# One transformer layer on one core: fewer seven-product groups in two weight blocks, and quarter sums moved from GpSimd to VectorE

## The chip, the core and the metric

The kernel runs on one core of a Trainium2 chip. The core has a matrix engine (TensorE, PE in the profile; its weight loads are PEld), three elementwise engines (VectorE = DVE, ScalarE = ACT, GpSimd = POOL), a queue engine that only issues transfers here (SyncE = SP), and 16 DMA engines that all queues share. The metric is the device time of one execution in microseconds, lower is better. Times below are from one profiled execution of the kernel before, and from three timed runs of it.

## The reference, cut to what matters

All arrays are float32. The sequence has 256 tokens, the model is 2048 wide, the feed-forward part 5632. The attention and retention heads are left out here, since the change does not touch them: `mixed` stands for what they give.

```
n = rmsnorm(h, norm_mix_w);  proj = n @ w_in
mixed = concat(attention(proj), retention(proj))     # 256 x 2048
h  = h + mixed @ w_out                               # 2048 x 2048
n2 = rmsnorm(h, norm_ffn_w)
h  = h + (silu(n2 @ w_gate) * (n2 @ w_up)) @ w_down  # 2048 x 5632, twice, and 5632 x 2048
y  = rmsnorm(h, norm_final_w)
```

## The kernel before

**Precision by halves.** Each float32 operand is split into a rounded part and the rest. A weight tile of 128 x 1024 is copied by ACT into the rounded half of a `ws` tile, and DVE subtracts to get the rest (`halved`, lines 529 to 532). PE then multiplies high with high, high with low and low with high, so every product is three matmuls (`three`, line 574). Five `ws` buffers exist.

**Blocks.** From 367 us on, the program is a row of blocks. Each multiplies the 256 tokens with a weight block of 1024 output columns: `o0` and `o1` for w_out, `gu0` to `gu10` for 512 columns of w_gate beside 512 of w_up, and `d0_0` to `d2_1` for w_down, in three groups. A block has 16 slices of 128 rows of the weights (12 in `d2_0` and `d2_1`). It is computed in two ways:

- An item `C` takes one slice classically: two halves of the tokens by two halves of the columns, 12 matmuls of 128 x 512, adding to the four results that are called 2, 3, 4 and 8 (PSUM banks).
- Four slices can be taken together by seven products in the manner of Strassen, items `1` to `7` of 6 matmuls each: 42 matmuls in place of 48. The letter `a` is the first four slices, `b` the next four. Item 1 loads three weight tiles, item 2 a fourth. Some products need sums of weight tiles: DVE adds two of them in place (`rawt`), and two are made by a DMA of POOL's queue that adds while it writes (`plus`, line 534). So seven tiles have to be halved, not four.

`M` (`mid`, line 666) combines the products 1, 5, 6 and 7 into four parts of 128 x 512, one ACT copy and four DVE operations. In `o0` and `o1` these parts are added to the residual `ht` by four DMAs of POOL's queue; in the `gu` blocks they stay. When a result's last matmul is done, one DVE operation of 128 x 512 ends it (`end_out`, `end_gu`); in `o0` and `o1` it needs the DMA of its part to have landed, and ACT then takes the sum of its squares.

**Activations.** `T` turns 128 x 512 pieces onto the feature axis: 8 transposes on PE, then copies to two tiles. In `o1` the two T's make `n2` of `ht0` and `ht1` (`turn_n2`), in `gu0` those of `ht2` and `ht3`, in later blocks T turns the gated output of the block before (`h2`). `H` gates: silu on ACT, one product on DVE. The seven products need sums of quarters of the activations as well, of 128 x 128 each (`pair_sums`, line 539): s5 = a22 - a21, s2 = a11 + s5, s3 = a11 - a21, s4 = a12 - s2. POOL makes these four, and the result `s` is halved into `sa`. That happens for the four tiles of the two T's in `o1`, and for two tiles in each of `gu1`, `gu2`, `gu5`, `gu6` and `gu9`: 14 tiles, 56 operations.

**What sets the order.** A string for each kind of block (`ORDERS`, lines 33 to 40) gives the order of its items by hand. `ch` chains each engine's instructions of the block stage in just this order. Before item k runs, the loads and halvings of the items up to three ahead have been written to the queues (`AHEAD = 3`). Work put on the list `later` (squares, the halving of `s`) is taken off one per item, behind the item. Raw weight tiles come from rings of buffers by home: three `rawc` (all C items and each item 1), three `raw22`, two `raw12`, one `rawt`. All loads are issued by SP in order, and a load waits until its buffer was read for the last time.

Of the kernel before, what the change touches and what calls it, by code (L numbers as in the profile page):

```python
# [12 lines left out]
ALU = mybir.AluOpType  # L13
# [4 lines left out]
S = 256  # L18
# [12 lines left out]
AHEAD = 3  # L31
MAIN = "1a 5a H 2a C T 3a C 6a C 7a 1b C 4a 5b C 2b 6b C 7b M C C 3b 4b"
ORDERS = {
# [3 lines left out]
    "main": MAIN,  # L37
    "short": "1a 5a H 2a C T 3a C 6a C 7a C M C 4a C C C",
    "final": "1a 5a 2a C 3a C 6a C 7a M C 4a K K K K Z",
# [49 lines left out]
def encoder_layer(ctx: ExitStack, tc: tile.TileContext, xT, x, gains, gain_f, decay, tab, w_qk, w_in, w_st, y):  # L89
# [8 lines left out]
    nc = tc.nc  # L98
# [10 lines left out]
    def atile(name):  # L109
        return actp.tile([P, 2, 2, S], F32R, tag="act", name=name)  # L110

    def ttile(name):
        return tmp.tile([P, 2, S], F32, tag="tmp", name=name)
# [152 lines left out]
    for c in range(KT // 2):  # L266
# [10 lines left out]
        a = atile(f"n1_{c}")  # L277
# [223 lines left out]
    queue, later = {}, []  # L501

    def ch_ins(ins):

        if ins.engine in queue:
            tc.add_manual_dep(
                ins, queue[ins.engine].name,
                mybir.DependencyInfo(mybir.DependencyClass.NoSync, mybir.DependencyReason.DATA), reason="stream",
            )
        queue[ins.engine] = ins  # L510

    def ch(ins):
        ch_ins(ins.ins)
# [9 lines left out]
    def copy(out, src, func=AF.Copy, **kw):  # L523
        ch(nc.scalar.activation(out, src, func, **kw))  # L524

    def tt(out, x, y, op):
        ch(nc.vector.tensor_tensor(out, x, y, op=op))  # L527

    def halved(to, src):

        copy(to[:, :, 0, :], src)
        tt(to[:, :, 1, :], src, to[:, :, 0, :].bitcast(F32), ALU.subtract)
# [6 lines left out]
    def pair_sums(t, name):  # L539
        s = ttile(f"s_{name}")  # L540
        a11, a21, a12, a22 = (t[:, f, i * P:(i + 1) * P] for f in range(2) for i in range(2))
        s5, s2, s3, s4 = (s[:, f, i * P:(i + 1) * P] for f in range(2) for i in range(2))
        for out, p, q, op in ((s5, a22, a21, ALU.subtract), (s2, a11, s5, ALU.add),
                              (s3, a11, a21, ALU.subtract), (s4, a12, s2, ALU.subtract)):
            ch(nc.gpsimd.tensor_tensor(out, p, q, op=op))  # L545
        a = atile(f"sa_{name}")
        later.append(lambda: halved(a, s))
        return a

    flat = "p f t -> p (f t)"  # L550
# [133 lines left out]
    def turn(t, name, dst, w=None, sums=None):  # L684

        for p in range(2):
            pt = halves(ps1(f"pt_{name}{p}"))
            for f in range(2):
                for i in range(2):
                    ch(nc.tensor.transpose(pt[:, f, i * P:(i + 1) * P], t(i)[:, (2 * p + f) * P:(2 * p + f + 1) * P], ident))  # L690
            a = atile(f"{name}_{p}")
            c = len(dst)
            dst.append(a)
            if sums is not None:
                o = ttile(f"o_{name}{p}")
                if w is None:
                    copy(o, pt)
                else:
                    for f in range(2):
                        copy(o[:, f], pt[:, f], scale=w[:, 2 * c + f:2 * c + f + 1])  # L700
                halved(a, o)
                sums.append(pair_sums(o, f"{name}_{p}"))
            elif w is None:
                halved(a, pt)
            else:
                for f in range(2):
                    g = w[:, 2 * c + f:2 * c + f + 1]
                    copy(a[:, f, 0, :], pt[:, f, :], scale=g)
                    ch(nc.vector.scalar_tensor_tensor(
                        a[:, f, 1, :], pt[:, f, :], g, a[:, f, 0, :].bitcast(F32), op0=ALU.mult, op1=ALU.subtract  # L710
                    ))
# [79 lines left out]
    for g, (lo, hi, s) in enumerate(GROUPS):  # L791
        h2, s2 = [], []
# [104 lines left out]
```

## Time and profile before

| what | value |
|---|---|
| median of three runs | 1191.64 us (1189.43 to 1192.74) |
| the profiled execution | 1192.01 us, of which the profile's span 1190.0 us |
| PE busy in the span | 96% |
| DVE busy | 82% |
| ACT, POOL busy | 57%, 21% |
| DMA engines, mean busy share in the slices of the block stage | 0.5 to 0.9 |
| input projection and heads | 0 to 367 us |
| `o0`, `o1`, `gu0` (by PE's first matmul) | from 367.0, 410.0, 459.1 us |
| `gu1` and the rest | from 518.4 us |

The span runs from the first to the last instruction that the profile shows; the 2.0 us beside it are outside the profile. Tile names are given without buffer numbers: `p_gu` is any of the result banks of any gu block, `raw_gu` a raw tile of the homes 22 and 12. In a timeline row the first number is the start in us, the second the time that the row takes, `x6` the number of instructions merged into it, and the bracket the idle time of the engine before it and what ended that.

### The profile page before, as it was taken

The page shows a single profiled execution, that of the slowest core. Times are in us where ns is not written, and L with a number is a line of the kernel's source. Part 1 is how long each engine was busy: PE and PEld are TensorE (multiplying, and loading weights), DVE is VectorE, ACT ScalarE, POOL GpSimd, SP SyncE. Part 2 cuts the span into 40 slices and gives each one's busy share as a digit, 9 for nine tenths or more (in the row PEclk, how much of TensorE's full clock was granted, in tenths as well). Part 3 has the DMA queues.
Part 4 walks back from the last instruction along what each step waited for, and adds up shares of the span by engine and source line. Part 5 has one row for each costly group of instructions (what it writes and reads, how often), then busy time and mean ns, then how long its engine had stood idle before and what let it go on. Part 6 is the DMA issues. An engine that isn't in the chain of part 4 may idle for free.

```text
span 1190.0 us, 15290 instructions
## 1 busy us (share of the span) xinstructions
PE 1140.6 (96%) x5534; PEld 950.0 (80%) x5534; DVE 977.8 (82%) x1007; ACT 681.2 (57%) x830; POOL 255.8 (21%) x258
## 2 busy tenths in 40 slices
PE   7999999999999987899999999999999999999996
PEld 5888888888887775677788878778788878878885
DVE  8887787667687787789898889789999878989985
ACT  5455555555555574546666645566666655656653
POOL 8332322203122251031300022032100112121011
PEclk9999999999999998899999999999999999999998
DMA  8665565554556968768788899978897899979785
GB/s 319 208 228 160 178 195 165 157 185 157 184 168 178 261 186 226 218 187 254 217 260 247 274 248 260 311 204 258 258 255 233 250 295 254 276 247 287 239 229 143
DMA packets 77691, 269.47 MB, mean 226 GB/s; under 512 B 8880, under 2 KB 8880, under 8 KB 77616
## 3 DMA queue, kind: packets, MB, share of 16 engines
q1 hardware_dynamic: 61920, 221.29, 53.8%
q0 software_dynamic: 14976, 46.14, 21.8%
q10 hardware_dynamic: 720, 1.07, 0.2%
q8 instruction: 43, 0.70, 0.2%
q14 instruction: 32, 0.26, 0.1%
HBM read 220.23 MB, written 2.10 MB: 187 GB/s over the span
## 4 chain that ended last, share of the span: by engine, by line
PE 74%; DVE 8%; DMA 6%; issue 4%; POOL 3%; ACT 3%; SPq 0%; DVEq 0%; POOLq 0%; ACTq 0%
PE p_gu L578 30%; PE p_d L578 15%; PE ps_qr L157 3%; PE ps_gr L157 3%; PE ps_vr L164 2%; PE ps_kr L157 2%; POOL s_h L545 2%; PE ps_va L164 2%; PE p_o L578 2%; PE ps_ka L157 2%; DVE ws_gu L527 2%; DMA rawc_d<-in_w_st 2%; DMA ht<-part_o 2%; PE ps_qa L157 2%; ACT ws_gu L524 1%
## 5 line engine op out<-in xcount | busy, mean ns | idle before, releaser
L578 PE MATMUL p_gu<-ws_gu,n 128*128 128x512 f32 x1452 | 352.0, 393 | 12.3 <-DVE ws_gu L527 9.0
L578 PEld LDWEIGHTS p_gu<-ws_gu,n 128*128 128x128 f32 x1452 | 273.7, 189 | 76.8 <-DVE ws_gu L527 14.7
L578 PE MATMUL p_d<-ws_d,h 128*128 128x512 f32 x708 | 168.6, 390 | 2.2 <-DVE ws_d L527 1.5
L578 PEld LDWEIGHTS p_d<-ws_d,h 128*128 128x128 f32 x708 | 132.8, 188 | 31.0 <-DVE ws_d L527 2.1
L527 DVE TENSOR_TENSOR ws_gu<-rawc_gu,ws_gu 128x1024 fp32r<-128x1024 f32 x110 | 134.4, 1222 | 26.1 <-ACT ws_gu L524 24.3
L524 ACT ACTIVATE ws_gu<-rawc_gu 128x1024 fp32r<-128x1024 f32 x110 | 115.7, 1056 | 49.1 <-PE p_gu L578 26.4
L578 PE MATMUL p_gu<-ws_gu,sa_n 128*128 128x512 f32 x528 | 136.4, 394 | 6.9 <-DVE ws_gu L527 4.4
L578 PEld LDWEIGHTS p_gu<-ws_gu,sa_n 128*128 128x128 f32 x528 | 98.9, 189 | 28.1 <-DVE ws_gu L527 4.7
L527 DVE TENSOR_TENSOR ws_gu<-raw_gu,ws_gu 128x1024 fp32r<-128x1024 f32 x88 | 107.5, 1222 | 5.5 <-ACT ws_gu L524 3.6
L524 ACT ACTIVATE ws_gu<-raw_gu 128x1024 fp32r<-128x1024 f32 x88 | 92.8, 1054 | 32.0 <-PE p_gu L578 24.0
L527 DVE TENSOR_TENSOR ws_d<-rawc_d,ws_d 128x1024 fp32r<-128x1024 f32 x54 | 65.7, 1220 | 18.9 <-ACT ws_d L524 18.1
L524 ACT ACTIVATE ws_gu<-rawt_gu 128x1024 fp32r<-128x1024 f32 x44 | 46.5, 1056 | 58.9 <-DVE rawt_gu L527 49.4
L524 ACT ACTIVATE ws_d<-rawc_d 128x1024 fp32r<-128x1024 f32 x54 | 57.2, 1059 | 35.5 <-PE p_d L578 18.9
L537 POOL DMA_DIRECT2D raw_gu<-raw_gu x22 | 19.1, 868 | 222.8 <-DVE rawt_gu L527 208.8
L578 PE MATMUL p_d<-ws_d,sa_h 128*128 128x512 f32 x240 | 61.2, 390 | 0.0
L527 DVE TENSOR_TENSOR ws_gu<-rawt_gu,ws_gu 128x1024 fp32r<-128x1024 f32 x44 | 53.7, 1220 | 5.6 <-ACT ws_gu L524 5.6
L578 PEld LDWEIGHTS p_d<-ws_d,sa_h 128*128 128x128 f32 x240 | 44.8, 188 | 9.2
L524 ACT ACTIVATE ws_d<-raw_d 128x1024 fp32r<-128x1024 f32 x40 | 42.3, 1056 | 14.2 <-PE p_d L578 12.7
L527 DVE TENSOR_TENSOR ws_d<-raw_d,ws_d 128x1024 fp32r<-128x1024 f32 x40 | 48.8, 1219 | 0.8
L578 PE MATMUL p_o<-ws_o,mr 128*128 128x512 f32 x192 | 46.6, 391 | 2.0 <-DVE ws_o L527 2.0
L537 POOL DMA_DIRECT2D raw_gu<-rawt_gu x22 | 19.0, 862 | 135.9 <-DVE ws_gu L527 135.9
L164 PE MATMUL ps_va<-ws_va,n 128*128 128x512 f32 x128 | 45.8, 400 | 0.0
(258 smaller groups left out, 2343.9 us busy)
## 6 DMA issues: line engine op xcount, KB each, us to landing
rawc_gu<-in_w_st SPq DMA_DIRECT2D x110, 512.0 KB, 5.4
raw_gu<-in_w_st SPq DMA_DIRECT2D x66, 512.0 KB, 5.5
rawc_d<-in_w_st SPq DMA_DIRECT2D x58, 512.0 KB, 4.9
raw_d<-in_w_st SPq DMA_DIRECT2D x30, 512.0 KB, 4.9
raw_gu<-raw_gu POOLq DMA_DIRECT2D x22, 512.0 KB, 7.6
raw_gu<-rawt_gu POOLq DMA_DIRECT2D x22, 512.0 KB, 5.7
rawc_o<-in_w_st SPq DMA_DIRECT2D x20, 512.0 KB, 4.5
raw_va<-in_w_in SPq DMA_DIRECT2D x16, 512.0 KB, 4.3
```

The source lines that it names most:

```text
L157: nc.tensor.matmul(ps[:, f, :], t[:, j, 0, f * P:(f + 1) * P], a, start=start, stop=False)
L164: nc.tensor.matmul(ps[:, f, :], a[:, 0, f * P:(f + 1) * P], t[:, j, :, :], start=first, stop=False)
L524: ch(nc.scalar.activation(out, src, func, **kw))
L527: ch(nc.vector.tensor_tensor(out, x, y, op=op))
L537: ch(nc.gpsimd.dma_start(out, other, accum_op=ALU.add))
L545: ch(nc.gpsimd.tensor_tensor(out, p, q, op=op))
L578: ch(nc.tensor.matmul(self.bank(r), x[u], w[v], start=r not in self.begun, stop=self.left[r] == 0))
```

## The change

Three things are edited.

First, in the strings of `o1` and `gu0` (kinds `out1` and `gu_first`) the seven products of the second four slices go, and four C items take their place: 7 products and 12 C items in a block, where there were 14 and 8. Each of the two blocks has 186 matmuls of 128 x 512 then, where it had 180, and 19 halvings and 2 DVE sums of weight tiles, where it had 22 and 4; two of the four DMA sums go as well. The T's and `M` stand at other places between the items. Second, the items of `o0` are the same ones in another order: `M` has 7 items behind it, not 4. Third, `pair_sums` does its four operations on DVE (by `tt`), and they are put on `later`, ahead of the halving of `s`.

```diff
-    "out0": "1a 5a 2a 3a S 6a 7a S 1b C 4a C 5b C 2b C 6b C 7b C M 3b C 4b C",
-    "out1": "1a 5a 2a C T 3a C T C 6a C 7a 1b 4a C 5b 2b C 6b C 7b M C 3b 4b",
-    "gu_first": "1a 5a 2a T 3a T 6a 7a 1b C 4a 5b C 2b C 6b C 7b C M C C 3b C 4b",
+    "out0": "1a 5a 2a 3a S 6a 7a S 1b C 5b 4a 6b C 2b C 7b M C 3b C C 4b C C",
+    "out1": "1a 5a 2a C 3a C T 6a C 7a C M C 4a C T C C C C C C",
+    "gu_first": "1a 5a 2a C T C C T C 3a 6a C 7a C 4a M C C C C C C",
...
     def pair_sums(t, name):
         s = ttile(f"s_{name}")
...
-        for out, p, q, op in ((s5, a22, a21, ALU.subtract), (s2, a11, s5, ALU.add),
-                              (s3, a11, a21, ALU.subtract), (s4, a12, s2, ALU.subtract)):
-            ch(nc.gpsimd.tensor_tensor(out, p, q, op=op))
         a = atile(f"sa_{name}")
-        later.append(lambda: halved(a, s))
+
+        def add():
+            for out, p, q, op in ((s5, a22, a21, ALU.subtract), (s2, a11, s5, ALU.add),
+                                  (s3, a11, a21, ALU.subtract), (s4, a12, s2, ALU.subtract)):
+                tt(out, p, q, op)
+
+        later.extend([add, lambda: halved(a, s)])
         return a
```

The first place is the seam from `o1` to `gu0` on DVE. `part..` is the work of `M`, `ht..` the four ends of `o1`, `ws_gu0` the halvings of gu0's first items. Before:

```order
L527 TENSOR_TENSOR v_o1_4086<-part0_o1_4082,p6_o1_3937 128x512
L674 SCALAR_TENSOR_TENSOR part2_o1_4084<-p5_o1_3767,v_o1_4086 128x512
L527 TENSOR_TENSOR part1_o1_4083<-p7_o1_3966,v_o1_4086 128x512
L527 TENSOR_TENSOR part3_o1_4085<-part2_o1_4084,p7_o1_3966 128x512
L527 TENSOR_TENSOR ws_gu0_4102<-rawc_gu0_4096,ws_gu0_4102 128x2x512
L527 TENSOR_TENSOR rawt_gu0_4105<-rawc_gu0_4096,raw12_gu0_4098 128x1024
L527 TENSOR_TENSOR ht2_3384<-p2_o1_3781,ht2_3384 128x512
L527 TENSOR_TENSOR ht3_3386<-p8_o1_3806,ht3_3386 128x512
L527 TENSOR_TENSOR ws_gu0_4124<-rawt_gu0_4105,ws_gu0_4124 128x2x512
```

And in the changed program (`s_n2` are the quarter sums of the second T of `o1`):

```order
L527 TENSOR_TENSOR s_n2_1_1_4011<-o_n2_11_4006,s_n2_1_1_4011 128x128
L527 TENSOR_TENSOR ws_gu0_4080<-rawc_gu0_4074,ws_gu0_4080 128x2x512
L527 TENSOR_TENSOR rawt_gu0_4083<-rawc_gu0_4074,raw12_gu0_4076 128x1024
L527 TENSOR_TENSOR sa_n2_1_1_4012<-s_n2_1_1_4011,sa_n2_1_1_4012 128x2x256
L527 TENSOR_TENSOR ws_gu0_4100<-rawt_gu0_4083,ws_gu0_4100 128x2x512
L527 TENSOR_TENSOR rawt_gu0_4083<-rawt_gu0_4083,raw22_gu0_4078 128x1024
L527 TENSOR_TENSOR ws_gu0_4118<-raw22_gu0_4116,ws_gu0_4118 128x2x512
L527 TENSOR_TENSOR ht2_3384<-p2_o1_3781,ht2_3384 128x512
L527 TENSOR_TENSOR ht3_3386<-p3_o1_3796,ht3_3386 128x512
L527 TENSOR_TENSOR ht2_3384<-p4_o1_3800,ht2_3384 128x512
L527 TENSOR_TENSOR ht3_3386<-p8_o1_3804,ht3_3386 128x512
L527 TENSOR_TENSOR ws_gu0_4142<-rawc_gu0_4140,ws_gu0_4142 128x2x512
```

`M` has moved from right ahead of the ends to eight C items ahead of them. All four ends now stand together, behind the halvings of items 1, 5 and 2 of `gu0` and ahead of that of its first C; before, they stood between those halvings.

The second place is the turns of `gu0` on DVE, where the `n2_2` and `n2_3` rows are the two T's and the `ws_gu0` rows halvings of the items around them. Before:

```order
L527 TENSOR_TENSOR ws_gu0_4164<-rawt_gu0_4105,ws_gu0_4164 128x2x512
L527 TENSOR_TENSOR ws_gu0_4174<-raw12_gu0_4098,ws_gu0_4174 128x2x512
L709 SCALAR_TENSOR_TENSOR n2_2_0_4189<-pt_n2_20_4184,nw_79,n2_2_0_4189 128x256 x2
L709 SCALAR_TENSOR_TENSOR n2_2_1_4199<-pt_n2_21_4194,nw_79,n2_2_1_4199 128x256 x2
L527 TENSOR_TENSOR ws_gu0_4210<-rawc_gu0_4204,ws_gu0_4210 128x2x512
L527 TENSOR_TENSOR rawt_gu0_4213<-rawc_gu0_4204,raw12_gu0_4206 128x1024
L709 SCALAR_TENSOR_TENSOR n2_3_0_4228<-pt_n2_30_4223,nw_79,n2_3_0_4228 128x256 x2
```

And in the changed program:

```order
L527 TENSOR_TENSOR ws_gu0_4156<-rawc_gu0_4154,ws_gu0_4156 128x2x512
L527 TENSOR_TENSOR ws_gu0_4170<-rawc_gu0_4168,ws_gu0_4170 128x2x512
L527 TENSOR_TENSOR ws_gu0_4184<-rawc_gu0_4182,ws_gu0_4184 128x2x512
L712 SCALAR_TENSOR_TENSOR n2_2_0_4207<-pt_n2_20_4202,nw_79,n2_2_0_4207 128x256 x2
L712 SCALAR_TENSOR_TENSOR n2_2_1_4217<-pt_n2_21_4212,nw_79,n2_2_1_4217 128x256 x2
L527 TENSOR_TENSOR ws_gu0_4222<-raw22_gu0_4078,ws_gu0_4222 128x2x512
L527 TENSOR_TENSOR ws_gu0_4237<-rawt_gu0_4083,ws_gu0_4237 128x2x512
L712 SCALAR_TENSOR_TENSOR n2_3_0_4257<-pt_n2_30_4252,nw_79,n2_3_0_4257 128x256 x2
L712 SCALAR_TENSOR_TENSOR n2_3_1_4267<-pt_n2_31_4262,nw_79,n2_3_1_4267 128x256 x2
L527 TENSOR_TENSOR ws_gu0_4274<-rawc_gu0_4272,ws_gu0_4274 128x2x512
```

The first T now has three halved C items behind it in stock and two C's between it and the second T; the second one has the halvings of items 3 and 6 ahead of it. Four C items in a row take their tiles from the three `rawc` buffers.

The third place is the T of `gu2` on DVE, one of the five later blocks with quarter sums. `h2` is the turned tile, `sa_h2` the halving of its sums. Before, DVE had none of the sums; they were eight rows on POOL, between two of its DMA sums:

```order
L527 TENSOR_TENSOR h2_1_1_4934<-o_h2_11_4935,h2_1_1_4934 128x2x256
L527 TENSOR_TENSOR ws_gu2_4947<-rawc_gu2_4945,ws_gu2_4947 128x2x512
L527 TENSOR_TENSOR sa_h2_1_0_4928<-s_h2_1_0_4923,sa_h2_1_0_4928 128x2x256
L527 TENSOR_TENSOR ws_gu2_4958<-raw12_gu2_4809,ws_gu2_4958 128x2x512
L527 TENSOR_TENSOR sa_h2_1_1_4944<-s_h2_1_1_4939,sa_h2_1_1_4944 128x2x256
L527 TENSOR_TENSOR ws_gu2_4981<-rawc_gu2_4975,ws_gu2_4981 128x2x512
L527 TENSOR_TENSOR rawt_gu2_4984<-rawc_gu2_4975,raw12_gu2_4977 128x1024
```

And in the changed program:

```order
L527 TENSOR_TENSOR ws_gu2_4923<-rawc_gu2_4921,ws_gu2_4923 128x2x512
L527 TENSOR_TENSOR s_h2_1_0_4907<-o_h2_10_4903 128x128
L527 TENSOR_TENSOR s_h2_1_0_4907<-o_h2_10_4903,s_h2_1_0_4907 128x128
L527 TENSOR_TENSOR s_h2_1_0_4907<-o_h2_10_4903 128x128
L527 TENSOR_TENSOR s_h2_1_0_4907<-o_h2_10_4903,s_h2_1_0_4907 128x128
L527 TENSOR_TENSOR ws_gu2_4936<-raw12_gu2_4793,ws_gu2_4936 128x2x512
L527 TENSOR_TENSOR sa_h2_1_0_4908<-s_h2_1_0_4907,sa_h2_1_0_4908 128x2x256
L527 TENSOR_TENSOR ws_gu2_4959<-rawc_gu2_4953,ws_gu2_4959 128x2x512
L527 TENSOR_TENSOR rawt_gu2_4962<-rawc_gu2_4953,raw12_gu2_4955 128x1024
L527 TENSOR_TENSOR s_h2_1_1_4919<-o_h2_11_4915 128x128
```

The sums of a tile stand on DVE one item ahead of its `sa` halving, and the second tile's come one weight halving and one weight sum later than its `sa` halving did.

## The prediction

> **What bounds the kernel now.** I read the page first (busy time by engine, costliest groups), then the chain that ended last, then PE's timeline for the gaps, and last the other engines' timelines at each gap.
>
> ```profile
> PE 1140.6 (96%) x5534; PEld 950.0 (80%) x5534; DVE 977.8 (82%) x1007; ACT 681.2 (57%) x830; POOL 255.8 (21%) x258
> ...
> L527 DVE TENSOR_TENSOR ws_gu<-rawc_gu,ws_gu 128x1024 fp32r<-128x1024 f32 x110 | 134.4, 1222 | 26.1 <-ACT ws_gu L524 24.3
> L524 ACT ACTIVATE ws_gu<-rawc_gu 128x1024 fp32r<-128x1024 f32 x110 | 115.7, 1056 | 49.1 <-PE p_gu L578 26.4
> ...
> 1124.47 49.70 PE p_d L578 x219
> ```
>
> PE is the bound on the whole, with DVE close behind. The last row, from the chain, gives PE's own pace: 49.70 / 219 = 0.227 us per matmul, so 1.36 us for a product item of 6 and 2.72 us for a C of 12. A halving costs DVE 1.22 us and ACT 1.06. A group of seven products is 7 x 1.36 = 9.52 us of PE and 9 DVE operations of 1.22 us (7 halvings, 2 sums), 10.98 us; four C's are 10.88 us of PE and only 4.88 of DVE. So a group saves PE 1.36 us only where DVE has the room.
>
> Where does PE stand still? In its timeline:
>
> ```profile
> 410.03 1.52 PE L578 MATMUL p_o<-ws_o,ma 128*128 128x512 f32 x6
> ...
> 416.47 2.83 PE L578 MATMUL p_o<-ws_o,mr 128*128 128x512 f32 x11 [1.97 <-DVE ws_o L527]
> ...
> 459.13 1.52 PE L578 MATMUL p_gu<-ws_gu,n 128*128 128x512 f32 x6
> ...
> 466.58 2.50 PE L578 MATMUL p_gu<-ws_gu,sa_n 128*128 128x512 f32 x5 [4.42 <-DVE ws_gu L527]
> ...
> 483.20 0.50 PE L578 MATMUL p_gu<-ws_gu,n 128*128 128x512 f32 x1 [2.98 <-ACT ws_gu L524]
> 484.46 6.90 PE L578 MATMUL p_gu<-ws_gu,n 128*128 128x512 f32 x17 [0.76 <-DVE ws_gu L527]
> ...
> 527.47 1.63 PE L578 MATMUL p_gu<-ws_gu,sa_n 128*128 128x512 f32 x6
> ```
>
> o1 begins at 410.03, gu0 at 459.13, and gu1's item 3, behind its T, at 527.47. These 117.44 us hold two blocks of 14 products and 8 C's (40.8 us each), two turns in each of 0.8 us (a gap-free T below ends 0.79 after its start), and gu1's 1, 5, 2, C, T (7.6): 92.4 us. **25.0 us are lost here**, the dearest stretch of the kernel. The reason of the largest gap, and the halves of a turn, on DVE:
>
> ```profile
> 464.70 0.69 DVE L527 TENSOR_TENSOR ht<-p_o,ht 128x512 f32<-128x512 f32 x1 [4.80 <-DMA ht<-part_o]
> ...
> 474.13 0.48 DVE L709 SCALAR_TENSOR_TENSOR n<-pt_n,nw,n 128x256 fp32r<-128x256 f32 x1
> 475.16 0.88 DVE L709 SCALAR_TENSOR_TENSOR n<-pt_n,nw,n 128x256 fp32r<-128x256 f32 x2 [0.54 <-ACT n L524]
> 476.57 0.48 DVE L709 SCALAR_TENSOR_TENSOR n<-pt_n,nw,n 128x256 fp32r<-128x256 f32 x1 [0.54 <-ACT n L524]
> ```
>
> An end of o1 waits 4.80 us for the DMA that M issued a few items earlier, with gu0's halvings queued behind it. Then two turns stand almost next to each other, and each holds DVE for 2.9 us (474.13 to 477.05) in turns with ACT. And the clock falls:
>
> ```profile
> 415.00:419.00 4.00, 2.53 (x11) 2.08 (x12) 4.00 (x5) 3.34 (x7) 0.00 (x0) 1.00 0.85 207
> ...
> 463.00:467.00 4.00, 0.42 (x1) 0.42 (x2) 2.27 (x3) 1.58 (x3) 0.00 (x0) 0.51 0.84 177
> ...
> 483.00:487.00 4.00, 3.04 (x7) 2.24 (x8) 3.79 (x4) 3.93 (x5) 0.00 (x0) 0.57 0.94 215
> ```
>
> The column before the last two is the granted clock: about half after the gaps of 4.42 and 2.98 us, full after that of 1.97. The 17 matmuls at 484.46 took 6.90 us in place of 3.86: a fall costs some 3.0 us.
>
> The second loss recurs. From one T's end to the next in gu2 and in gu3 on PE, and then DVE in gu2, with a row of the waits at its end:
>
> ```profile
> 571.73 1.62 PE L578 MATMUL p_gu<-ws_gu,sa_n 128*128 128x512 f32 x6
> ...
> 582.68 1.64 PE L578 MATMUL p_gu<-ws_gu,n 128*128 128x512 f32 x6 [0.76 <-DVE ws_gu L527]
> 584.95 4.19 PE L578 MATMUL p_gu<-ws_gu,n 128*128 128x512 f32 x17 [0.63 <-DVE ws_gu L527]
> ...
> 615.62 1.63 PE L578 MATMUL p_gu<-ws_gu,sa_n 128*128 128x512 f32 x6
> ...
> 656.57 1.03 PE L690 MATMUL pt_h<-ident,part_gu 128*128 128x128 f32 x8
> 657.36 1.62 PE L578 MATMUL p_d<-ws_d,sa_h 128*128 128x512 f32 x6
> ```
>
> ```profile
> 577.21 0.82 DVE L527 TENSOR_TENSOR sa_h<-s_h,sa_h 128x512 fp32r<-128x512 f32 x1 [1.02 <-ACT sa_h L524]
> ...
> 580.45 0.69 DVE L527 TENSOR_TENSOR sa_h<-s_h,sa_h 128x512 fp32r<-128x512 f32 x1 [1.02 <-ACT sa_h L524]
> ...
> 583.68 1.22 DVE L527 TENSOR_TENSOR ws_gu<-rawc_gu,ws_gu 128x1024 fp32r<-128x1024 f32 x1
> ...
> ACT sa_h L524 <- POOL s_h L545: 16.4, 10, 1.7
> ```
>
> gu2, with quarter sums, takes 615.62 - 571.73 = 43.89 us; gu3, without, 657.36 - 615.62 = 41.74, PE's full pace. ACT waits for POOL's sums (ten times, up to 1.7 us, the last row, from the waits), DVE for ACT, and the C behind 1b comes late. **2.15 us in each of five blocks, 10.75 in all.**
>
> **The change, part by part.** *PE's work.* Two groups become eight C's: +2 x 1.36 = 2.72 us.
>
> *M earlier.* Now a C and two products (5.4 us) lie between M and o1's last end, and the end waits 4.80 more: the DMA sums take some 10 us. In the new o1 8 C's and a product lie there, over 22 us. The wait goes, with the fall of the clock behind it. In o0 seven items (16.3 us) lie there in place of four (8.2), so most of the 1.97 us goes. The new order of o0's other items I cost at nothing: three products in a row take 4.1 us of PE against 3.7 of DVE, and halvings stand in stock; if not, some tenths.
>
> *Four ends at once.* One block in the trace ends so already, d2_0, with a row of C's behind its M (PE, ACT, DVE):
>
> ```profile
> 1133.87 16.48 PE L578 MATMUL p_d<-ws_d,h 128*128 128x512 f32 x72
> 1150.19 1.52 PE L578 MATMUL p_d<-ws_d,sa_h 128*128 128x512 f32 x6
> ...
> 1139.97 1.06 ACT L524 ACTIVATE ws_d<-rawc_d 128x1024 fp32r<-128x1024 f32 x1 [2.11 <-DMA rawc_d<-in_w_st]
> ...
> 1148.17 2.48 DVE L527 TENSOR_TENSOR ht<-p_d,ht 128x512 f32<-128x512 f32 x4
> ```
>
> PE runs through without a gap, though item 1's tile waited 2.11 us for its load: the halving was still 6 us early. That is the model, with one doubt, since o1's end is fuller.
>
> *The walk through o1's end.* What is late next is the ring of three rawc buffers:
>
> ```profile
> rawc_gu<-in_w_st SPq DMA_DIRECT2D x10, 512.0 KB, 5.1
> ...
> rawc_o<-in_w_st SPq DMA_DIRECT2D x8, 512.0 KB, 5.8
> ...
> rawc_d<-in_w_st SPq DMA_DIRECT2D x13, 512.0 KB, 4.7
> ```
>
> A buffer turns in 5.1 (landing near this place) + 1.06 + 1.22 = 7.4 us. I count from o1's start on PE; its end, without a gap, is at 9.52 + 12 x 2.72 + 1.6 = 43.8. The first T ends at 11.7, DVE gets past its halvings at 15.3, and then has, without a pause, four halvings, two sums of quarters, two sa, M and the next C's halving: about 11.4 us, to 26.7. That buffer's next two turns end at 34.1 and 41.5: the last is item 1 of gu0. Behind it in DVE's queue stand a sum, sa, item 5, a sum, item 2, each halving behind its ACT copy: item 2 is ready at 47.4, while PE needs it at 43.8 + 2.7 = 46.5: 0.9 us. Then the ends, late too, and gu0's first C, whose ACT copy stands behind the first end's square: 0.69 + 0.63 + 1.04 + 1.22 = 3.6 behind item 2, against 1.36 of PE: 2.2 us. So **3.1 us at gu0's head**. Further on, the fourth C takes the buffer of the first (7.4), and behind its halving DVE has turn 2.9, item 3 1.8, item 6 1.1, turn 2.9 and the next C 1.8: that C is ready 17.9 us after the first began, PE's work until then is 15.2: **2.7 us at the second T**. I add 0.5 for places where halvings end within 0.2 us of their need. With landings of 4.7 or 5.8 the 5.8 us become 4.6 or 7.9; d2_0's row as the model makes them 0.
>
> Sum of the stretch: 43.8 + 43.8 + 7.6 + 6.3 = 101.5 in place of 117.4: **-15.9 us**. That counts gu1's gate without its present gap, since the four ends come as results finish; if that gap stays, it is up to 1.5 more.
>
> *Sums on DVE.* No 128 x 128 operation on DVE stands in the trace; the nearest:
>
> ```profile
> 373.53 0.16 DVE L217 TENSOR_SCALAR ms_r<-pm_r 128x4 f32<-128x4 f32 x1
> ...
> 378.37 0.88 DVE L483 SCALAR_TENSOR_TENSOR ort<-ort,nw,g 128x256 f32<-128x256 f32 x2
> ```
>
> So 0.16 to 0.44 us each. From 128x512 at 0.69 and 128x1024 at 1.22 the line gives 0.29, of which 0.09 overlaps where no result is waited for (the four ends of d2_0 take 2.48 together, at 0.69 each), and two of the four wait for one: about 0.95 for four, 1.9 for a block. In gu2 DVE stood waiting for sa 2 x 1.02 and some tenths more, so the sums fill about that time, and by the order the halving of the C behind 1b ends at 583.3 (now 584.9) where PE wants it at 582.8: 0.5. DVE is then some 41 us busy in a block of 41.7, so I put the loss at 0.8 per block: 5 x (2.15 - 0.8) = **-6.75 us**. At 0.16 it is 0.5 less per block (-9); at 0.44, 1.6 more (+1). What POOL is rid of gains nothing by itself: it is idle four fifths of the span.
>
> The Trainium skill, VectorE: DVE Perf Modes, section The DRAIN you can't avoid, says against this that the next DVE operation does not start until the pipe has emptied, and asks for fewer operations. By it four sums cost 4 x 0.29 = 1.16, some 2 us more in all, 1171. The ends' row speaks for some overlap: 4 x 0.69 is 2.76, and they took 2.48.
>
> Total: 1192.0 (the profiled execution, span 1190.0 and 2.0 around it; the runs' median is 0.4 below) - 15.9 - 6.75 = 1169.4: **1169 us**.
>
> **Rivals.**
> *A, the clock falls at gu0.* The gaps of 2.2 and 2.7 us lie between 1.97 (no fall) and 2.98 (fall). One fall gives 1172, two 1175. The Trainium skill, TensorE: Matmul & The Clock Gate, section What's actually happening, has the clock halved after an idle window of about 3.4 us; by that neither gap would do it. The trace does not quite agree: the clock fell after 2.98 us as well.
> *B, no new gaps.* The seam goes as in d2_0 and the sums hide whole: -(15.9 + 6.3) - 10.75 gives 1159. Against it stands the fuller DVE queue.
> *C, the sums move nothing.* DVE, at 0.44 each or through its order, becomes the bound in the five blocks, as late as POOL made it: 1169 + 6.75 = 1176, and to 1180 with the four sums of o1, which lie ahead of the 26.7 and of item 1. For it: DVE is nearly full there. This is the change not doing what it says.
> *D, the loads become the bound.* The two blocks draw 26 tiles through three buffers, (landing + 2.3) / 3 each. Now the two take 49.10 + 59.28 = 108.4 us; with the sums' 6.75 gained, the kernel is 3.6 us slower (0.3%, what a measurement can tell) when the 26 take 118.7, so from a landing of 11.4 us: 1195.6.
>
> ```profile
> 952.86 10.99 DMA rawc_d<-in_w_st
> ```
>
> Single loads have waits of that size, where DMA sums crowd the queues; but two DMA sums of weights fewer run in each of the two blocks, and the medians are half of it.
>
> **How the numbers follow.** Forecast 0.42, A 0.22, B 0.16, C 0.10, D 0.10 (half of it slower, half within 0.3%). The predicted time is the forecast's. The range goes from B's 1159 less one to C's 1180 and leaves out D, 0.10: 1158 to 1180. All but D are faster by over 1%: 0.90, within 0.3% 0.05, slower 0.05.
>
> **What would show it.** Right: no ht end waits for a DMA; the stretch from o1's start to gu1's item 3 is 98 to 105 us; gaps of 2 to 3 us at gu0's first C and at the C behind its item 6; gu2 takes 42 to 43 us; four DVE sums take about 0.95. Wrong: gu2 still at 43.9, clock rows near 0.5 in gu0, a rawc wait ahead of most C's, or new gaps in o0.

## The result and the profile after

| kernel | median of the runs | ratio to before, 95% interval |
|---|---|---|
| before, in the same session | 1190.61 us | 1 |
| the change | 1171.63 us (1170.53 to 1173.20, four runs) | 0.984 (0.9819 to 0.986) |

The forecast was 1169 us and the range 1158 to 1180. The profiled execution took 1173.20 us, 18.8 less than that of before, and it was the slowest of the four. Its page:

```profile
span 1171.0 us, 15265 instructions
PE 1139.8 (97%) x5546; PEld 953.4 (81%) x5546; DVE 971.2 (83%) x1053; ACT 673.4 (58%) x824; POOL 202.2 (17%) x198
```

PE is busy as long as before (1140.6) in a span that is 19 us shorter: what went is standing still. PE's timeline from o1's first item to gu1's turn, cut to the rows with a gap, gu0's second turn, the C behind its item 6, and the two ends of the stretch:

```profile
410.38 1.52 PE L581 MATMUL p_o<-ws_o,ma 128*128 128x512 f32 x6
415.06 0.49 PE L581 MATMUL p_o<-ws_o,ma 128*128 128x512 f32 x1 [0.43 <-ACT ws_o L524]
416.31 2.79 PE L581 MATMUL p_o<-ws_o,ma 128*128 128x512 f32 x11 [0.77 <-DVE ws_o L527]
...
424.56 1.66 PE L581 MATMUL p_o<-ws_o,sa_ma 128*128 128x512 f32 x6 [0.49 <-ACT o_n L524]
...
460.81 1.45 PE L581 MATMUL p_gu<-ws_gu,n 128*128 128x512 f32 x5 [0.74 <-DVE ws_gu L527]
463.11 0.51 PE L581 MATMUL p_gu<-ws_gu,n 128*128 128x512 f32 x1 [0.86 <-ACT ws_gu L524]
464.37 4.39 PE L581 MATMUL p_gu<-ws_gu,n 128*128 128x512 f32 x11 [0.76 <-DVE ws_gu L527]
...
474.93 1.04 PE L693 MATMUL pt_n<-ident,ht 128*128 128x128 f32 x8
...
481.29 2.88 PE L581 MATMUL p_gu<-ws_gu,n 128*128 128x512 f32 x12
...
511.11 2.81 PE L581 MATMUL p_gu<-ws_gu,n 128*128 128x512 f32 x11 [0.87 <-DVE ws_gu L527]
514.86 0.33 PE L693 MATMUL pt_h<-ident,part_gu 128*128 128x128 f32 x1 [0.94 <-DVE part_gu L758]
515.52 0.98 PE L693 MATMUL pt_h<-ident,part_gu 128*128 128x128 f32 x7 [0.33 <-DVE part_gu L758]
...
516.26 1.63 PE L581 MATMUL p_gu<-ws_gu,sa_n 128*128 128x512 f32 x6
```

From o1's start to gu1's item 3 it is 516.26 - 410.38 = 105.88 us, where it was 117.44 and I had put 101.5. The gaps stand at three heads: o1's first C and turn (1.7 us), gu0's item 2 and first C (2.4), gu1's C and gate (2.1). The rows of gu0's second turn and of the C behind its item 6 have none. The row at 464.37 also shows a slow clock: 11 matmuls in 4.39 us, where 11 take 2.8 elsewhere. The granted clock, in the windows view of the same run (the column before the last two):

```profile
459.00:463.00 4.00, 2.51 (x10) 1.40 (x8) 4.00 (x6) 1.61 (x4) 0.86 (x1) 1.00 0.81 165
463.00:467.00 4.00, 3.13 (x8) 2.30 (x9) 3.33 (x4) 3.79 (x9) 0.00 (x0) 0.71 0.89 218
467.00:471.00 4.00, 4.00 (x21) 3.34 (x20) 2.06 (x3) 1.81 (x3) 0.00 (x0) 0.86 0.70 253
```

DVE's timeline at gu0's head and at gu1's, cut to item 1, the four ends and the C that follows them, with the halving of the C behind gu0's item 6 (479.47) between the two heads:

```profile
453.59 1.22 DVE L527 TENSOR_TENSOR ws_gu<-rawc_gu,ws_gu 128x1024 fp32r<-128x1024 f32 x1
...
460.67 2.47 DVE L527 TENSOR_TENSOR ht<-p_o,ht 128x512 f32<-128x512 f32 x4
463.09 1.23 DVE L527 TENSOR_TENSOR ws_gu<-rawc_gu,ws_gu 128x1024 fp32r<-128x1024 f32 x1
...
479.47 1.23 DVE L527 TENSOR_TENSOR ws_gu<-rawc_gu,ws_gu 128x1024 fp32r<-128x1024 f32 x1 [0.46 <-ACT ws_gu L524]
...
500.06 1.22 DVE L527 TENSOR_TENSOR ws_gu<-rawc_gu,ws_gu 128x1024 fp32r<-128x1024 f32 x1 [2.88 <-ACT ws_gu L524]
...
507.45 2.48 DVE L527 TENSOR_TENSOR part_gu<-p_gu,part_gu 128x512 f32<-128x512 f32 x4
```

No end waits for a DMA any more; the four run in one piece of 2.47. But they come late, as they stand in DVE's queue behind the halvings of a new block's items 1, 5 and 2, and item 1 comes late itself. Why, ACT's timeline in gu0's tail of six C's says:

```profile
488.12 1.06 ACT L524 ACTIVATE ws_gu<-rawc_gu 128x1024 fp32r<-128x1024 f32 x1 [2.85 <-DMA rawc_gu<-in_w_st]
...
491.73 1.06 ACT L524 ACTIVATE ws_gu<-rawc_gu 128x1024 fp32r<-128x1024 f32 x1 [1.12 <-DMA rawc_gu<-in_w_st]
...
494.87 1.06 ACT L524 ACTIVATE ws_gu<-rawc_gu 128x1024 fp32r<-128x1024 f32 x1 [2.07 <-DMA rawc_gu<-in_w_st]
...
498.97 1.06 ACT L524 ACTIVATE ws_gu<-rawc_gu 128x1024 fp32r<-128x1024 f32 x1 [3.04 <-DMA rawc_gu<-in_w_st]
```

The last of these is gu1's item 1: each of the four waits for its load to land. The sums and a block that has them, gu2, in DVE's and PE's timelines:

```profile
563.17 0.28 DVE L527 TENSOR_TENSOR s_h<-o_h 128x128 f32<-128x128 f32 x1
563.49 0.29 DVE L527 TENSOR_TENSOR s_h<-o_h,s_h 128x128 f32<-128x128 f32 x1
563.70 0.28 DVE L527 TENSOR_TENSOR s_h<-o_h 128x128 f32<-128x128 f32 x1
563.90 0.28 DVE L527 TENSOR_TENSOR s_h<-o_h,s_h 128x128 f32<-128x128 f32 x1
564.10 1.22 DVE L527 TENSOR_TENSOR ws_gu<-raw_gu,ws_gu 128x1024 fp32r<-128x1024 f32 x1
```

```profile
557.99 1.04 PE L693 MATMUL pt_h<-ident,part_gu 128*128 128x128 f32 x8
600.15 1.03 PE L693 MATMUL pt_h<-ident,part_gu 128*128 128x128 f32 x8
```

Four sums hold DVE for 564.10 - 563.17 = 0.93 us, and gu2 takes 600.15 - 557.99 = 42.16 from turn to turn, against 43.89.

### The profile page after: what moved, and what is told of

Read it like the earlier page. It is cut to its first block, busy times and chain, and to the rows that moved or that the text cites. A ratio compares the mean times of both kernels' runs of the same rounds, so it can differ in the third digit from the quotient of the medians.

```text
span 1171.0 us, 15265 instructions
## 1 busy us (share of the span) xinstructions
PE 1139.8 (97%) x5546; PEld 953.4 (81%) x5546; DVE 971.2 (83%) x1053; ACT 673.4 (58%) x824; POOL 202.2 (17%) x198
## 4 chain that ended last, share of the span: by engine, by line
PE 74%; DVE 12%; DMA 7%; issue 4%; ACT 3%; POOL 0%; SPq 0%; DVEq 0%; POOLq 0%; ACTq 0%
PE p_gu L581 29%; PE p_d L581 13%; DVE ws_gu L527 3%; DMA rawc_d<-in_w_st 3%; PE ps_qr L157 3%; PE ps_va L164 3%; PE ps_gr L157 3%; PE ps_vr L164 3%; PE ps_kr L157 3%; PE p_o L581 2%; PE ps_ka L157 2%; DMA rawc_gu<-in_w_st 2%; PE ps_qa L157 2%; DMA rawc_o<-in_w_st 1%; DVE ws_o L527 1%
## 5 line engine op out<-in xcount | busy, mean ns | idle before, releaser
L581 PE MATMUL p_gu<-ws_gu,n 128*128 128x512 f32 x1482 | 355.9, 392 | 6.4 <-DVE ws_gu L527 4.8
L581 PEld LDWEIGHTS p_gu<-ws_gu,n 128*128 128x128 f32 x1482 | 278.4, 188 | 69.1 <-DVE ws_gu L527 8.9
L527 DVE TENSOR_TENSOR ws_gu<-rawc_gu,ws_gu 128x1024 fp32r<-128x1024 f32 x113 | 137.7, 1220 | 29.2 <-ACT ws_gu L524 28.0
L524 ACT ACTIVATE ws_gu<-rawc_gu 128x1024 fp32r<-128x1024 f32 x113 | 118.8, 1056 | 53.5 <-PE p_gu L581 28.6
L581 PE MATMUL p_gu<-ws_gu,sa_n 128*128 128x512 f32 x504 | 128.5, 391 | 0.0
L581 PEld LDWEIGHTS p_gu<-ws_gu,sa_n 128*128 128x128 f32 x504 | 93.9, 188 | 19.2 <-DVE ws_gu L527 0.2
L527 DVE TENSOR_TENSOR ws_gu<-raw_gu,ws_gu 128x1024 fp32r<-128x1024 f32 x84 | 102.4, 1219 | 1.5 <-ACT ws_gu L524 0.5
L524 ACT ACTIVATE ws_gu<-raw_gu 128x1024 fp32r<-128x1024 f32 x84 | 88.5, 1054 | 22.3 <-PE p_gu L581 18.5
L524 ACT ACTIVATE ws_d<-raw_d 128x1024 fp32r<-128x1024 f32 x40 | 42.2, 1055 | 12.6 <-PE p_d L581 11.4
L157 PE MATMUL ps_gr<-n,ws_gr 128*128 128x512 f32 x128 | 45.6, 399 | 0.0
L157 PE MATMUL ps_qr<-n,ws_qr 128*128 128x512 f32 x128 | 45.5, 399 | 0.0
```

The source lines that it names most:

```text
L157: nc.tensor.matmul(ps[:, f, :], t[:, j, 0, f * P:(f + 1) * P], a, start=start, stop=False)
L581: ch(nc.tensor.matmul(self.bank(r), x[u], w[v], start=r not in self.begun, stop=self.left[r] == 0))
```

## The experiments

The time of each is the median of four runs (five for e10), the ratio is to the kernel before in the same session. "Stretch" below is from o1's first matmul to the first transpose of gu1's turn, 1.4 us less than the stretch of the prediction: 116.0 us before (526.07 - 410.03), 104.5 with the change (514.86 - 410.38).

**e1 and e2, one part each.** e1 is the new kernel with `pair_sums` as it was; e2 the kernel before with the new `pair_sums` and the old strings.

> The new orders with the sums as before (GpSimd, at once). If the two parts simply add, the sums are worth the 8.6 us read from the later trace (five blocks, each 42.16 to 42.21 us from T to T instead of 43.86), so this runs at 1171.6 + 8.6 = 1180 us (1178.5 to 1181.5), and gu2, gu5, gu6 and gu9 are back at 43.8 us from T to T. Rival: the sums of o1's two turns on VectorE also carry part of the stretch from o1 to gu1, or cost it; then it comes out above 1183 or below 1177, and the stretch is not the 105.9 us it has with both parts.

> The old orders with the new sums (VectorE, put off). Theory: 1190.6 - 8.6 = 1182 us (1180.5 to 1184), T to T in gu2, gu5 and gu6 42.2 us, the stretch from o1's start to gu1's item 3 within 1 us of its 117.4. Rival: the sums are worth something only beside the new orders, or nothing: 1188 us and more.

e1: 1182.24 us, 0.9918 (0.9901 to 0.9935), stretch 104.0. e2: 1181.91 us, 0.9914 (0.9897 to 0.9932), stretch 115.3. e2 came as its theory had it, and e1 lies 0.7 us above its band and below the rival's. 0.9918 x 0.9914 is 0.9833, and both together gave 0.984: **the two parts add**, some 10 us each. The sums do next to nothing in the stretch (104.0 against 104.5), and the orders gain nothing outside it. In e1's profile they even lose there: gu1 takes 47.68 us from turn to turn, where it took 44.87 before, with gaps of 0.53 and 1.32 us near its end. Of the 12.0 us that e1 gains in the stretch, 8.9 are left in its profiled execution. With the new sums gu1 loses nothing by the orders (43.13 us with the change, 43.09 in e2). Whether e1's loss there comes again in other executions is not shown by one profile.

**e4 and e6, fourteen products in o1, M early.**

```diff
-    "out1": "1a 5a 2a C 3a C T 6a C 7a C M C 4a C T C C C C C C",
+    "out1": "1a 5a 2a C 3a C T 6a C 7a 1b C 5b 6b C 7b M C 4a T C 2b C 3b 4b",      (e4)
+    "out1": "1a 5a 2a C 3a C T 6a C 7a 1b C 5b 2b 6b C 7b M C 4a T C 3b C 4b",      (e6)
```

> The new kernel with o1's fourteen products and eight C's put back, but M ahead of the last eleven items and the two turns apart. Theory A (M's place and the turns' spacing are what pays): the second group takes 1.36 us off PE again, so 1169.5 to 1172 us, with no end that waits for a DMA. Theory B (fewer products pay, as they leave VectorE room): a second group asks 10.98 us of VectorE in place of 4.88 within o1, gu0's item 1 is halved later than 44.4 us after o1's start, and the time is 1174 to 1179 us.

e4: 1183.64 us, 0.993 (0.9912 to 0.9949), slower than either theory had. POOL's queue and ACT's wait in its trace:

```profile
444.87 2.64 POOL L537 DMA_DIRECT2D ht<-part_o  x3 [2.85 <-DVE part_o L527]
446.60 1.79 POOL L537 DMA_DIRECT2D raw_o<-rawt_o  x1
```

```profile
459.02 1.06 ACT L524 ACTIVATE ws_o<-raw_o 128x1024 fp32r<-128x1024 f32 x1 [8.31 <-DMA raw_o<-rawt_o]
```

The DMA sum that item 4 needs was issued right behind M's sums into ht and landed only at 459 us: M's transfers hold up the one behind them in the queue. That is a price of an early M in a block that still has a second group, which neither theory had. e6 takes it away by putting item 2 ahead of M (and item 3 ahead of the last C):

> The kernel of e4 with item 2 of the second group ahead of M, so that its accumulating transfer no longer stands behind M's four (in e4 it was issued at 446.60 us, right behind them, and item 4 waited 8.31 us for it). Fourteen products in o1, M early, turns apart. Theory B1 (e4 was slow through that queue alone, the number of products matters little): ACT's wait of 8.31 us is gone and the time is 1169 to 1174 us. Theory B2 (fewer products pay in themselves, VectorE's room): item 1 of gu0 is halved later than 44.4 us after o1's start and the time is 1175 to 1180 us.

e6: 1177.19 us, 0.9874 (0.9852 to 0.9897). The wait of 8.31 us is gone. The time is B2's, but its sign is small: item 1 of gu0 is halved 45.2 us after o1's start (454.16 + 1.22 - 410.16), where the new kernel has 44.4, and the stretch is 106.4, only 1.9 longer. It holds a gap of 3.45 us at gu0's item 2, and there another cause stands: by e6's string three of the ends (1.88 us), and the last sums of the second turn, put off (0.93 us), come ahead of that halving on DVE:

```profile
460.10 1.88 DVE L527 TENSOR_TENSOR ht<-p_o,ht 128x512 f32<-128x512 f32 x3
461.90 0.28 DVE L527 TENSOR_TENSOR s_n<-o_n 128x128 f32<-128x128 f32 x1
...
462.83 1.22 DVE L527 TENSOR_TENSOR ws_gu<-raw_gu,ws_gu 128x1024 fp32r<-128x1024 f32 x1
```

The rest of its loss in the profile, some 3 us, is a fall of the clock in gu4 (at 740 us) and small gaps in the d blocks. So whether seven products pay in themselves is **left open** by e6.

**e3 and e5, M late.** e3 moved o1's M alone, to ahead of its last C, and gave no time: its instructions wait for one another in a ring (a deadlock). From item 7 until M all eight result banks are taken, and e3 has a turn between the two. So with M late both turns have to stand ahead of item 7; e5 puts them ahead of item 6, as they were before the change, and by that moves the turns as well as M.

```diff
-    "out1": "1a 5a 2a C 3a C T 6a C 7a C M C 4a C T C C C C C C",
+    "out1": "1a 5a 2a C 3a C T C C T 6a C 7a C C 4a C C C M C C",
```

> The new kernel with o1's M behind nine of its C's and two C's ahead of the end, which is the 5.4 us ahead of the end at which M stood before; the turns stand ahead of item 6, two C's apart. Still seven products. Theory: the four accumulating transfers land after o1's last C, its ends wait some 4 to 5 us for a DMA with gu0's halvings behind them on VectorE, the granted clock falls there, and the stretch from o1's start to gu1's item 3 takes 111 to 115 us: 1176 to 1181 us. Rival: with seven products fewer halvings stand behind the ends, so the wait falls into time that VectorE has to spare: 1170 to 1173 us, though a row shows the wait.

e5: 1173.97 us, 0.9848 (0.9826 to 0.9869), stretch 107.9. The mechanism is there, in DVE's and then PE's timeline:

```profile
461.18 0.69 DVE L527 TENSOR_TENSOR ht<-p_o,ht 128x512 f32<-128x512 f32 x1 [3.26 <-DMA ht<-part_o]
463.69 1.97 DVE L527 TENSOR_TENSOR ht<-p_o,ht 128x512 f32<-128x512 f32 x3 [1.82 <-DMA ht<-part_o]
```

```profile
463.63 0.50 PE L581 MATMUL p_gu<-ws_gu,n 128*128 128x512 f32 x1 [3.44 <-ACT ws_gu L524]
466.85 5.06 PE L581 MATMUL p_gu<-ws_gu,n 128*128 128x512 f32 x11 [2.72 <-DVE ws_gu L527]
```

Yet the median is only 2.3 us above the change's, and the intervals overlap; in the stretch late M costs 3.4 us. The 6.2 us of gaps are not all M's: with the change PE loses 2.4 us at the same place, with a slow clock behind it as well. So e5 stands 3.8 us longer there, and at gu1's C it has no gap, where the change has 0.87. The theory priced late M as if the change had no gaps there.

**e7, two rings for the last C's.** e5 and ACT's waits point to the ring of three `rawc` buffers. The C's 11, 13 and 15 of o1 and gu0 go into the ring of the items 2 and 3, which is idle there:

```diff
-                return self.halve(self.load("c"))
+                return self.halve(self.load("22" if self.late and m in (11, 13, 15) else "c"))
```

with `self.late = kind in ("out1", "gu_first")`.

> The new kernel with every second of the last six C's of o1 and gu0 loaded into the ring that items 2 and 3 have left, so that these C's have two rings in place of one of three. Theory (the turn of the one ring makes the next block's item 1 late, and with it the ends and the halving behind them): ACT's waits for a C's load in gu0's tail, 9.1 us in four in the run of the change, fall to under 3; gu1's item 1 is halved 2 us earlier or more; the gaps at gu0's and gu1's heads shrink by 2 to 5 us together: 1167 to 1170 us. Rival (the transfers themselves are the limit: more of them in flight only land later): landings stretch from 4.3 to 6 us and more, and the time stays within 1.5 us of 1171.6.

e7: **1163.92 us**, 0.9767 (0.9744 to 0.979), stretch 97.3, 7.2 less than with the change. PE has no gap at gu0's and gu1's heads, ACT waits for no load from o1 to gu1's turn, and no clock falls there. Its DVE timeline at gu1's head:

```profile
491.17 1.23 DVE L527 TENSOR_TENSOR ws_gu<-rawc_gu,ws_gu 128x1024 fp32r<-128x1024 f32 x1 [1.49 <-ACT ws_gu L524]
...
498.92 1.37 DVE L527 TENSOR_TENSOR part_gu<-p_gu,part_gu 128x512 f32<-128x512 f32 x2 [0.56 <-PE p_gu L582]
```

Item 1 comes 8.8 us earlier after o1's start (80.9 instead of 89.7), and the ends now wait for PE, not the other way round. Landings of rawc_gu grew from 4.3 to 4.9 us (medians between 440 and 505 us): the transfers weren't the limit, the number of buffers was.

**e9, M late with two rings.** e7 with e5's string.

> e7 (the last C's of o1 and gu0 on two rings) with o1's order of e5 (M late, turns ahead of item 6). Late M cost only 1 to 2 us on the new kernel (e5), though the ends waited 3.26 and 1.82 us for a DMA there and gu0's first C came 6.2 us late. Theory: that loss was hidden, since the loads, bound by the one ring, caught up in the pause; with two rings nothing is left to catch up, and late M costs what its gaps show, 5 to 8 us over e7: 1169 to 1172 us. Rival: late M is worth 1 to 2 us here too: 1165 to 1167 us.

e9: 1168.87 us, 0.9816 (0.9802 to 0.9829), stretch 102.3, both 5.0 above e7. So M's place, with the turns', is worth 5 us where the ring isn't short; where it is, 3.4 in the stretch. That the loads make up in the pause what they would have been late by is not shown: in gu0's tail ACT waits 9.2 us for loads in e5 and 9.1 with the change. The difference is in what stood at gu0's head already. The change has gaps and a slow clock there with M early, too; e7 has neither, so that in e9 late M pays for the whole gap and for the fall of the clock (4.36 us for 11 matmuls, 1.6 more than at full clock). This gap of 2.80 us and the slow clock behind it are what is left in e9's stretch beside the gaps in o1 (0.54, 0.76 and 0.74):

```profile
464.15 4.36 PE L582 MATMUL p_gu<-ws_gu,n 128*128 128x512 f32 x11 [2.80 <-DVE ws_gu L527]
```

**e10, two rings in o0 as well.** `self.late` holds for `out0` too, where it moves the C's 11, 13 and 15 (the expectation names two of the three).

> e7 with o0's C's 13 and 15 on the second ring as well. In e7, ACT still waits 3.41 us for the load of o1's item 1 (at 403.87 us), item 1 is halved only at 404.96, item 2 at 410.93, and the four ends stand between it and the first C: the last gaps of the stretch are 0.42 and 0.76 us at o1's first C and 0.49 at its first turn. Theory: they have the same cause as gu0's had, so they shrink by 1 to 1.7 us: 1162 to 1163 us. Rival: o0's fourteen products keep the second ring busy, so the C's land no earlier there and item 1's own tiles of that ring later: 1164 to 1168 us.

e10: **1162.61 us** (1161.87 to 1163.42), 0.9765 (0.9751 to 0.9778), stretch 96.1. The two gaps at o1's first C are gone, that at the turn (0.49) stays, and one of 0.22 us shows at gu0's C behind item 6. The 1.2 us are in the trace; as times, e10 and e7 can't be told apart. Both beat the change.

**e8, four items ahead.** `AHEAD = 4` for 3.

> The new kernel with every item prepared four items ahead instead of three. Theory: the first C's halving then stands ahead of the four ends on VectorE at each block's head, so the gaps at the first C of o1 (1.2 us) and of gu0 (1.6 us, with the fall of the clock 1.9 more) go: 1167 to 1170 us. Rival: ACT and VectorE, which work in order, now wait at a load one item earlier, with turns, squares and ends queued behind; in the stretches where the one ring of three is late this costs more than it gives: 1173 to 1185 us.

e8: 1199.56 us, 1.0073 (1.0049 to 1.0096), slower than before, and above the rival's range, too. The stretch went as the theory had it, 100.7, 3.8 less than with the change. What it costs lies outside: gu2 and gu3 take 44.6 us each, with sums or without, the turn of each waiting for the gate. DVE's timeline there:

```profile
552.95 1.22 DVE L527 TENSOR_TENSOR ws_gu<-rawc_gu,ws_gu 128x1024 fp32r<-128x1024 f32 x1
554.09 1.41 DVE L758 SCALAR_TENSOR_TENSOR part_gu<-part_gu,r,part_gu 128x512 f32<-128x512 f32 x2
```

One more halving stands ahead of the gate's product on an engine that has no idle time in these 10 us (546 to 557 us); that this order alone makes the 2.5 to 2.9 us a block was not tried apart.

**e11 and e12, engine or place of the sums.** e11 leaves them put off but gives them to POOL; e12 leaves them on DVE but does them at once.

> The new kernel with the quarter sums put off as they are now, but on GpSimd. Theory (the engine is what pays): four sums take GpSimd 3.7 us in the run of before (818 and 1050 ns each), put off by an item they are ready later still, and ACT waits for them: 1181 to 1187 us. Rival (being put off is what pays, as it takes the sums from between a turn and the next halving): 1171 to 1174 us.

> The new kernel with the quarter sums on VectorE, but at once behind their turn's halving instead of an item later. Theory (the engine is all of it): within 1.5 us of 1171.6. Rival (place on VectorE matters): the sums of both halves of a turn, 0.93 us each, stand ahead of halvings that PE waits for, and each of the five blocks with sums loses 0.5 to 1.9 us more: 1174 to 1181 us.

e11: 1178.81 us, 0.9895 (0.9882 to 0.9909), 2 us below its theory and far above the rival. e12: 1170.38 us, 0.9826 (0.9813 to 0.984), as the theory had it. **The engine pays**; putting the sums off gains nothing on DVE: gu2 takes 42.04 us in e12, 42.16 with the change, 43.47 in e11. ACT's waits for the sums (total, times, longest), of e11 and then of the change:

```profile
ACT sa_h L524 <- POOL s_h L548: 26.0, 10, 4.5
```

```profile
ACT sa_h L524 <- DVE s_h L527: 18.4, 10, 2.4
```

ACT waits long in both, yet with the change gu2 is only 0.44 us above gu3, which has no sums: most of that wait lies beside other work. e11 against e1, that is what putting off gains on POOL, stays unclear, since the intervals overlap.

**e13, gu0's order alone put back.**

> The new kernel with gu0's order alone put back (fourteen products, both turns ahead of item 6, one item apart). Theory: the gaps behind the turns come back (2.98 and 0.76 us in the run of before, 3.0 for the clock, 1.4 at the second turn's item), less 1.36 for the second group of products and the 2.9 us that are lost at gu1's head now, where before lost 1.5: 1174 to 1178 us. Rival A: what the old gu0 lost came from o1's late ends, which o1's new order has removed, so that its own order costs nothing: 1169 to 1172 us. Rival B: gu0's order carries nearly all of the stretch's gain, o1's nothing: 1180 us and more.

e13: 1176.11 us, 0.9876 (0.9859 to 0.9892), stretch 107.5. PE's timeline shows the old gaps in smaller form:

```profile
467.46 4.46 PE L581 MATMUL p_gu<-ws_gu,sa_n 128*128 128x512 f32 x12 [2.32 <-DVE n L712]
...
474.87 0.50 PE L581 MATMUL p_gu<-ws_gu,n 128*128 128x512 f32 x1 [1.57 <-ACT ws_gu L524]
476.13 5.79 PE L581 MATMUL p_gu<-ws_gu,n 128*128 128x512 f32 x17 [0.76 <-DVE ws_gu L527]
```

Of the stretch's 11.5 us, 3.0 (107.5 - 104.5) go when gu0's order is undone; the other 8.5 stay, with o0's and o1's orders. What e13's profile loses beyond these 3 us lies behind the stretch, about half of it a slow clock in d1_1. Both rivals are out.

## Why the prediction was right, and where it was off

- **PE's work** and **o0's order** came as put: o0 takes 410.38 - 367.26 = 43.1 us, before 43.0.
- **M earlier**: the wait of 4.80 us is gone, as was said. Its share of the gain, with the turns' places, is 3.4 us of the stretch in this kernel (e5; 2.3 by the medians, whose intervals overlap) and 5.0 where the ring isn't short (e9).
- **The walk through o1's end** was right in kind and too kind by 3 us: the three ends of halvings that I put at 26.7, 34.1 and 41.5 us after o1's start came at 28.5, 38.0 and 44.4. 1.8 was late ahead of the ring (o1's head, which I took to be clean, has 1.7 us of gaps), 1.1 in its two turns, where loads took up to 8.6 us to land, not 5.1. The gaps at gu0's head were put at 3.1 and measured 0.74 + 0.86 + 0.76 = 2.4. The 2.7 at the second turn did not come, and not because the walk was wrong there: the halving of the C behind item 6 was ready 17.6 us after the first C's start (479.47 + 1.23 - 463.11), where I had 17.9. It was PE that came late. I had 15.2 us for its way from the first C to that one, and it took 18.2 (481.29 - 463.11), with the gap of 0.76 and the slow clock on it. So the fall of the clock took the place of this gap and did not come on top of it, which the prediction did not weigh.
- **The step that failed** is the sentence that the four ends "come as results finish" at gu1's gate, and d2_0 as the model for a head without a gap. They came behind a late item 1: 2.1 us of gaps at gu1's head, where I had 0 and "up to 1.5 more", and 1.7 at o1's, where I had 0. e7 and e10 show the cause: with more buffers for the C's of the tail ahead, the gaps at gu0's and gu1's heads and at o1's first C go. d2_0's six C's have the same ring; its halving was 6 us early there, and that is what the model took over without ground.
- **Rival D**, the ring, was weighed as all or nothing, with a point from which it makes the kernel slower (landings of 11.4 us). It took part at landings of 4.3 us: it cost 7.2 us of the stretch (what e7 gains), and left the kernel faster all the same.
- **Rival A**, the clock: one fall, some 1.7 us by the two windows at 463 us (4 x 0.29 + 4 x 0.14 = 1.7) and 1.6 by the rows (4.39 - 2.79). A had put 3.0 for it, from 17 matmuls in 6.90 us against 3.86; but a row of 17 at full clock takes 4.19 (584.95 in the prediction), so that fall had cost 2.7.
- **The sums**: four take 0.93 us (put: 0.95). The loss in a block fell to 0.44 (42.16 against gu3's 41.72), where I had 0.8, so gu2, gu5, gu6 and gu9 gained some 1.7 each, 8.5 us with gu1, not 6.75.

In sum: -11.6 in the stretch (put: -15.9), -8.5 from the sums (put: -6.75), and +1.3 elsewhere, among it a gap of 0.34 in d2_1 that wasn't there: -18.8 in the profiled execution. The errors of the stretch (4.3) and of the sums (1.75) were of opposite sign, so that the total came closer than the stretch alone: that part is luck.

## What to carry to other kernels

An order that gives a whole tail to one kind of item gives it to one ring of buffers: count the ring's turns, landing and release, against the pace of the tail, and let an idle ring help before anything is reordered. A gap's width is not what its removal pays: ask what stands at the same place without it, and test it by removing that first (M's place was worth 3.4 us of the stretch, and 5 once the ring was eased). A queue of DMA sums is an order too: what is put ahead in it makes the next one late, as in e4.

## What the runs showed of the hardware

**The same gaps, and the clock falls or doesn't.** At gu0's head the change has gaps of 0.74, 0.86 and 0.76 us, e1 gaps of 0.73, 0.87 and 0.76, e12 gaps of 0.25, 0.87 and 0.76. Behind them 11 matmuls took 4.39 us with the change, 2.79 in e1 and 4.38 in e12. The windows of e1, then of e12 (PE's busy time is the second number, the granted clock the last but two); those of the change stand above:

```profile
459.00:463.00 4.00, 1.94 (x7) 1.05 (x7) 3.94 (x6) 2.99 (x6) 0.86 (x1) 1.00 0.76 146
463.00:467.00 4.00, 4.00 (x22) 3.41 (x23) 2.45 (x2) 2.91 (x7) 0.00 (x0) 1.00 0.78 221
```

```profile
459.00:463.00 4.00, 2.29 (x8) 1.05 (x6) 4.00 (x6) 2.82 (x6) 0.86 (x1) 1.00 0.85 171
463.00:467.00 4.00, 3.83 (x10) 3.03 (x11) 2.57 (x3) 2.59 (x6) 0.00 (x0) 0.57 0.78 232
```

PE stood still longer in e1, and e12's clock fell. It is the same with a single gap of 1.86 us at gu1's C: 11 matmuls took 2.83 us behind it in e11, and 4.38 in e12. So no width of gap decides it here, and a term for the clock is a chance of some 1.6 us (4.38 - 2.79) at each place with such gaps. The Trainium skill, TensorE: Matmul & The Clock Gate, section What's actually happening, says that the activity is judged in a free-running window of about 3.4 us; that would make the same gaps fall differently from run to run, and these rows agree with it. It also says that the clock falls after an idle window; here it fell with PE busy 2.29 of 4 us, in gaps that are 1.9 us together. The measurement decides: a window without any work was not needed.

**Here DVE operations overlap where they don't read the one before.** Each of the four sums takes 0.28 to 0.29 us. The second reads the first's result and starts 0.32 after it; the third and the fourth don't read the operation just ahead of them and start after 0.21 and 0.20, while it still runs. The Trainium skill, VectorE: DVE Perf Modes, section The DRAIN you can't avoid, has the next operation start only when the pipe is empty, and adds that one which is not held starts earlier. These rows agree with the addition: 0.93 us for four, not the 1.16 that the prediction worked out by the rule.
